# Two decoder layers on one core: attention in rounds between dense products, shared PSUM banks, inverse roots on GpSimd

## The chip, the cores and the metric

The kernel runs on one core of a Trainium2 chip, in one launch. The metric is the device time of that launch in microseconds (us); the kernel before took 696.32 us in the median of three runs (696.04 to 697.86).

In the rows PE is TensorE's matmuls and PEld its weight loads, DVE is VectorE, ACT is ScalarE, POOL is GpSimd, and SP is SyncE, which issues the loads. L221 is line 221 of the kernel.

## The reference

Two layers work on 256 tokens of 1024 features. Each layer is: a mixer, a squared-ReLU MLP, and a per-layer input gated into the residual. Layer 0's mixer is two attentions side by side, layer 1's is one.

```python
def rms_norm(x, g):
    xf = x.astype(jnp.float32)
    y = xf * lax.rsqrt(jnp.mean(xf * xf, axis=-1, keepdims=True) + EPS)
    return (y * g.astype(jnp.float32)).astype(x.dtype)
...
    for i in range(DEPTH):
        hn = rms_norm(h, mix_norm[i])
        mix = even_mixer(...) if i % 2 == 0 else odd_mixer(...)
        h = h + mix
        u = jax.nn.relu(rms_norm(h, ff_norm[i]) @ w_ff1[i])
        h = h + (u * u) @ w_ff2[i]
        g = jax.nn.sigmoid(rms_norm(h, ple_norm[i]) @ w_ple_gate[i])
        h = h + g * (p[i] @ w_ple_proj[i])
```

The even mixer has eight heads of latent attention (MLA: compressed queries of 384 and keys and values of 256, both normalised, heads of 64 plus a rotary part of 32, causal) and eight heads of dilated attention (heads of 64). The odd mixer has 16 heads of 64; with 256 tokens there is one block, so it is causal attention with a distance bias. Queries and keys of every head are normalised by the root of their mean square, and softmax runs over up to 256 keys.

## The kernel before, in words

Every dense product is done in three passes of a reduced fp32 type: weights and activations are split into a high and a low part (`split`, L109 to L111: ScalarE copies the high part, VectorE subtracts it), and high by high, high by low and low by high are added up in PSUM. Weights come in chunks of about 1 MB, in the order of a list; `take` hands out the next chunk and has the two after it loaded and split, a piece of 512 columns at a time, in three buffers.

Activations are feature-major (`feat_mm`, L221: 256 columns to a matmul) or token-major (`tok_mm`, L233: up to 512). Queries, keys and values are token-major products. `heads_norm`, `mla_queries` and `mla_keys` square them on ScalarE, sum on VectorE, take the inverse root (`rsqrt`, L86 to L102), scale, and return a call that transposes the heads on TensorE (`transpose4`, L255) in groups of four, evicted by ScalarE or VectorE.

`rsqrt` is ScalarE's Sqrt, VectorE's reciprocal and, where asked, four more VectorE steps that refine it. Sqrt and Exp are in different tables of ScalarE, so going from one to the other loads a table.

`attn_pair` (L290 to L337) does two heads: their scores in two PSUM banks (L297, L299), bias and row minimum on VectorE (L306), Exp on ScalarE, the row's division on VectorE (L321), three transposes to a head through the one bank named tr (L324), copied by ScalarE (L326), and the products with the values in the bank named o (L330, L333), the first head into rows 0 to 63, the second into rows 64 to 127. Heads of 64 lie two to a tile, in rows 0 to 63 and 64 to 127; MLA heads have 96 rows from row 0. PSUM is 4 banks for dense products (pool pm), 2 for scores (pa), 1 for transposes (pt), 1 for values (po).

What stands in which order on an engine is decided by a scheduler that goes by its own estimate of what is ready first; only the start of layer 0, up to the sums of squares of the residual (L505 to L534), is in written order. The whole attention of a mixer is written behind its products, the per-layer input's projection (`embed`) and the output projection behind it, and the scheduler mixes them.

Of the kernel before, what the change touches and what calls it, by code (L numbers as in the profile page):

```python
# [50 lines left out]
def trunk(ctx, tc, xT, pT, pos, cst, vec, w_c, w_kv, w_dil, w_uq, w_ukv, w_eo,  # L51
# [12 lines left out]
    pt = ctx.enter_context(tc.tile_pool(name="pt", bufs=1, space=PS))  # L64
    po = ctx.enter_context(tc.tile_pool(name="po", bufs=1, space=PS))
# [11 lines left out]
    # the clock gate opens while the first loads are on their way  # L77
# [5 lines left out]
    eps = cp.tile([P, 1], F32, name="eps")  # L83
    V.memset(eps, EPS)

    def rsqrt(y, src, n, refine=False):  # L86
        """y = (src / n + EPS) ** -0.5; n: a number, or one for each src[:, :, i];
        refine: a Newton step on the square root's reciprocal."""
        shp = list(y.shape)
        t = tp.tile(shp, F32, tag=f"nt{shp}", name="nt", bufs=1 if shp[-1] == S else 2)  # L90
        if refine:
            m = tp.tile(shp, F32, tag=f"nm{shp}", name="nm")
# [6 lines left out]
        if refine:  # L99
# [18 lines left out]
    # weights in the order of their use, emitted ahead of it  # L118
# [42 lines left out]
    class Norm:  # L161
        """Gain, split and square sums of the residual, pair of chunks by pair."""
# [40 lines left out]
        def cols(self):  # L203
            """1/rms of every token on all partitions, [128, 256]."""
# [4 lines left out]
            rsqrt(r, ps, D)  # L209
# [5 lines left out]
    def feat_mm(ps, n, wt, x, k0, nk, total, done):  # L215
        """Feature-major: ps[:, j, :] += W[:, tile j].T @ x for k0..k0+nk."""
# [10 lines left out]
    def tok_mm(pss, n, wt, x, k0, nk, total, done):  # L227
        """Token-major: pss[t] += x[:, tokens of t].T @ W for k0..k0+nk."""
# [9 lines left out]
    def tok_group(x, n, nk, kper, late={}, pool=None):  # L238
        """Token-major product; late[i]: calls made before chunk i."""
# [11 lines left out]
    def transpose4(dst, srcs, rows, gain):  # L251
        """Four [128, rows] sources -> dst [rows, 4, 128], times gain."""
# [37 lines left out]
    def attn_pair(heads, mask, mult, dst_hi, dst_lo):  # L290
        """heads: two of (qT [K,256], kT [K,256], v0 [128,64], v1 [128,64], slope)."""
        pts = []
# [7 lines left out]
        for s, (_, _, _, _, slope) in zip(ss, heads):  # L300
# [3 lines left out]
            pr = tp.tile([P, 384], F32, tag="pr", name="pr", bufs=3)  # L304
# [15 lines left out]
            for t, sl in enumerate((slice(0, P), slice(P, 384))):  # L320
                V.tensor_scalar_mul(pr[:, sl], pr[:, sl], rd[:, t:t + 1])  # L321
            ps = pt.tile([P, 384], F32, tag="tr", name="tr")
            for i in range(3):
                T.transpose(ps[:, i * P:(i + 1) * P], pr[:, i * P:(i + 1) * P], ident)  # L324
            pT_ = tp.tile([P, 384], F32, tag="pT", name="pT", bufs=3)
# [10 lines left out]

    def big(shape, dt=F32, name="big"):  # L337
        return bp.tile(shape, dt, tag="b4", name=name)

    def out_proj(mixed, nxt):  # L340
        pss = [pm.tile([P, 2, S], F32, tag="mm", name="mm") for _ in range(4)]
        for kh in range(2):
            for nh in range(2):
                wh, wl = take()
                for j in range(2):
                    c = 2 * nh + j
                    sl = slice(j * 256, (j + 1) * 256)
                    feat_mm(pss[c], 2, (wh[:, :, sl], wl[:, :, sl]), mixed,
                            4 * kh, 4, 8, 4 * kh)
        for c in range(4):  # L350
            hp_ = h[:, 2 * c:2 * c + 2, :]
            V.tensor_add(hp_, pss[c], hp_)
            nxt.pair(c)

    def embed(layer):
        """The per-layer input's projection, feature-major."""
# [5 lines left out]
        es = [big([P, 4, S], name="ple") for _ in range(2)]  # L362
# [5 lines left out]
        return es  # L368
# [121 lines left out]
    def rope(dst, x, tab, t, nh):  # L490
        """dst, x [128, nh, 32]; dst = rotated x."""
# [44 lines left out]
    # gain columns  # L536
# [6 lines left out]
    def compress(pss, n, goff, name):  # L543
        """RMS-normalised latent; the call returned transposes and splits it."""
# [32 lines left out]
    def mla_queries(pss, qT):  # L577
        """Four heads: normalised, rotated; the call returned transposes them."""
# [8 lines left out]
        rsqrt(rs, ms, (64, 32), True)  # L587
# [17 lines left out]
    def mla_keys(pss, kTs):  # L605
        """Eight heads with the shared rotary part; the call returned transposes them."""
# [7 lines left out]
        rsqrt(rs, ms, 64, True)  # L614
# [25 lines left out]
    def rotary_key():  # L640
        kr = tp.tile([P, 2], F32, tag="kr", name="kr", bufs=1)
        rsqrt(kr, km, 32, True)
# [15 lines left out]
    # dilated queries  # L658
# [5 lines left out]
    # MLA queries, keys, values; then dilated keys and values  # L664
# [12 lines left out]
    pss = tok_group(x0, 512, 8, 4, {0: [q0_fin]})  # L677
    dk = big([P, 4, S], name="dk")
    dk_fin = heads_norm(pss, r0, dk, vc[:, V_DK:V_DK + 1])
    pss = tok_group(x0, 512, 8, 4, {0: [q1_fin], 1: [mk_fin, dk_fin]})  # L680
    dv = big([P, 2, 512], name="dv")
    values(pss, r0, dv)

    causal = cs[:, C_CAUSAL:C_CAUSAL + 384]
    for j in range(4):
        hs = []
        for i in range(2):
            hd = 2 * j + i
            sl = slice(hd * 64, (hd + 1) * 64)
            hs.append((mq[hd // 4][:96, hd % 4, :], kTs[hd // 4][:96, hd % 4, :],  # L690
                       mv[:, 0, sl], mv[:, 1, sl], 1.0))
        attn_pair(hs, causal, None, mixed[0][:, j, :], mixed[1][:, j, :])


    def head_pairs(q, k, v, slopes, mask, mult, base):
        for j in range(4):
            hs = []
            for i in range(2):
                hd = 2 * j + i
                sl = slice(hd * 64, (hd + 1) * 64)  # L700
                pr = slice(i * 64, (i + 1) * 64)
                hs.append((q[pr, j, :], k[pr, j, :], v[:, 0, sl], v[:, 1, sl], slopes[hd]))
            attn_pair(hs, mask, mult, mixed[0][:, base + j, :], mixed[1][:, base + j, :])

    head_pairs(dq, dk, dv, [2.0 ** -(i + 1) for i in range(8)],
               cs[:, C_DIL:C_DIL + 384], cs[:, C_MULT:C_MULT + 384], 4)

    es = embed(0)
    nf = Norm(V_FF)
    out_proj(mixed, nf)  # L710
# [5 lines left out]
    # ================= layer 1 =================  # L716
    r1 = None
    x1 = (n1.hi, n1.lo)
    mixed = new_x()
    fin = []  # L720
    for g in range(2):
        pss = tok_group(x1, 512, 8, 4, {1: fin})
        if g == 0:
            r1 = n1.rows()
        q = big([P, 4, S], name="oq")
        fin = [heads_norm(pss, r1, q, goq[:, 4 * g:4 * g + 4])]
        pss = tok_group(x1, 512, 8, 4, {1: fin})
        k = big([P, 4, S], name="ok")
        fin = [heads_norm(pss, r1, k, vc[:, V_OK:V_OK + 1])]
        pss = tok_group(x1, 512, 8, 4, {1: fin})  # L730
        fin = []
        v = big([P, 2, 512], name="ov")
        values(pss, r1, v)
        head_pairs(q, k, v, [2.0 ** (-(8 * g + i + 1) / 2.0) for i in range(8)],
                   cs[:, C_DIST:C_DIST + 384], None, 4 * g)
    es = embed(1)
    nf = Norm(V_FF + 8)
    out_proj(mixed, nf)
# [91 lines left out]
```

## Time and profile before

| what | value |
|---|---|
| median of 3 runs | 696.32 us (696.04 to 697.86) |
| span of the profiled execution | 695.1 us |
| TensorE busy | 684.3 us (98%) |
| VectorE busy | 454.0 us (65%) |
| ScalarE busy | 402.1 us (58%) |
| GpSimd busy | 7.8 us (1%) |
| granted TensorE clock, mean | 0.997 |
| bytes moved | 114.19 MB, 164 GB/s |

The profile gives the span from the first to the last instruction of one execution; the run's time, with what lies around the span, is in the runs, whose median stands 1.2 us above this span. A TensorE that is busy 98% can still be spending time between products: the ends of matmuls are modelled, and a matmul that waits for the one before counts as busy. So the distance from start to start is what counts. The chain of waits gives the work that ended last in order of time: start, duration, engine, what was made and the line.

### The profile page before, as it was taken

Reading aid. Unit: us, or ns where it says so; the run is one execution under the profiler, and the core shown is the slowest. Engines: PE = TensorE matmul, PEld = TensorE weight load, DVE = VectorE, ACT = ScalarE, POOL = GpSimd, SP = SyncE. Lnnn points to the kernel's source line nnn. Section 1 sums busy time; section 2 is a strip of 40 time slices with the busy share of each in tenths; the row PEclk is TensorE's granted clock in tenths of the full one; section 3 lists DMA queues with packets and bytes.
Section 4 is the critical chain, followed back from the end, with each engine's and each line's share of the span. In section 5 each row is a group of like instructions: output and inputs, shape, how many; then the busy total and the mean of one; then the engine's idle time right before and its main releaser. Section 6 shows DMA issues by size and latency. Waiting matters only on the chain.

```text
span 695.1 us, 12543 instructions
## 1 busy us (share of the span) xinstructions
PE 684.3 (98%) x5014; PEld 632.3 (91%) x5014; DVE 454.0 (65%) x1012; ACT 402.1 (58%) x833; POOL 7.8 (1%) x28
## 2 busy tenths in 40 slices
PE   8989999999999999999999999999999999999997
PEld 7878867999999999999988678689999999999997
DVE  5799678686645546557888657648765465564674
ACT  6876776575534435446765765756654354453551
POOL 3100000000000000000000000000000000000000
PEclk9999999999999999999999999999999999999999
DMA  8563610545555554545455235144555545555411
GB/s 257 210 238 136 243 62 5 182 173 188 183 182 182 186 182 178 188 177 183 159 204 182 70 112 197 62 136 167 182 182 190 183 174 194 175 179 197 166 62 61
DMA packets 19066, 114.19 MB, mean 164 GB/s; under 512 B 2240, under 2 KB 4672, under 8 KB 6208
## 3 DMA queue, kind: packets, MB, share of 16 engines
q1 hardware_dynamic: 19008, 113.40, 46.0%
q8 instruction: 39, 0.64, 0.4%
q14 instruction: 19, 0.16, 0.1%
HBM read 112.34 MB, written 1.05 MB: 163 GB/s over the span
## 4 chain that ended last, share of the span: by engine, by line
PE 94%; DVE 2%; DMA 2%; ACT 1%; issue 0%; SPq 0%; POOL 0%; DVEq 0%; ACTq 0%
PE mm L221 42%; PE f L221 27%; PE mm L233 15%; PE o L330 2%; PE tr L324 2%; PE s L299 2%; PE s L297 1%; PE tr L255 1%; DMA raw<-w_c 1%; DMA raw<-w_dil 1%; PE o L333 1%; DVE lo L111 1%; PE st L207 0%; ACT sq L550 0%; ACT L95 0%
## 5 line engine op out<-in xcount | busy, mean ns | idle before, releaser
L110 ACT ACTIVATE hi<-raw 128x512 fp32r<-128x512 f32 (+2 forms) x418 | 241.0, 622 | 212.2 <-PE mm L221 99.9
L111 DVE TENSOR_TENSOR lo<-raw,hi 128x512 fp32r<-128x512 f32 (+2 forms) x418 | 271.5, 685 | 109.6 <-ACT hi L110 109.2
L221 PE MATMUL f<-xh,hi 128*128 128x256 f32 x512 | 145.3, 284 | 0.0
L221 PE MATMUL mm<-uh,hi 128*128 128x256 f32 x512 | 144.9, 283 | 0.0
L221 PE MATMUL mm<-ul,hi 128*128 128x256 f32 x512 | 144.9, 283 | 0.0
L221 PE MATMUL mm<-uh,lo 128*128 128x256 f32 x512 | 144.9, 283 | 0.0
L221 PE MATMUL f<-xh,lo 128*128 128x256 f32 x512 | 144.9, 283 | 0.0
L221 PE MATMUL f<-xl,hi 128*128 128x256 f32 x512 | 144.9, 283 | 0.0
L221 PEld LDWEIGHTS f<-xl,hi 128*128 128x128 f32 x512 | 98.3, 192 | 0.1
L221 PEld LDWEIGHTS f<-xh,hi 128*128 128x128 f32 x512 | 98.3, 192 | 0.1
L221 PEld LDWEIGHTS mm<-uh,hi 128*128 128x128 f32 x512 | 98.3, 192 | 0.0
L221 PEld LDWEIGHTS mm<-ul,hi 128*128 128x128 f32 x512 | 98.3, 192 | 0.0
L221 PEld LDWEIGHTS mm<-uh,lo 128*128 128x128 f32 x512 | 98.3, 192 | 0.0
L221 PEld LDWEIGHTS f<-xh,lo 128*128 128x128 f32 x512 | 98.3, 192 | 0.0
L221 PE MATMUL mm<-xh,hi 128*128 128x256 f32 x256 | 73.0, 285 | 0.0
L221 PE MATMUL mm<-xl,hi 128*128 128x256 f32 x256 | 73.0, 285 | 0.0
L221 PE MATMUL mm<-xh,lo 128*128 128x256 f32 x256 | 72.8, 285 | 0.0
L233 PE MATMUL mm<-hi,xh 128*128 128x512 f32 (+1 forms) x160 | 63.3, 398 | 1.2 <-ACT hi L110 1.2
L233 PE MATMUL mm<-lo,xh 128*128 128x512 f32 (+1 forms) x160 | 63.2, 395 | 0.5 <-DVE lo L111 0.5
L233 PE MATMUL mm<-hi,xl 128*128 128x512 f32 (+1 forms) x160 | 62.5, 390 | 0.0
L391 DVE SCALAR_TENSOR_TENSOR u<-f,cr 128x512 f32<-128x512 f32 x32 | 22.1, 691 | 52.4 <-PE f L221 52.4
L221 PEld LDWEIGHTS mm<-xh,hi 128*128 128x128 f32 x256 | 49.0, 192 | 0.8 <-issue 0.8
(189 smaller groups left out, 876.1 us busy)
## 6 DMA issues: line engine op xcount, KB each, us to landing
raw<-w_f SPq DMA_DIRECT2D x64, 1024.0 KB, 4.8
raw<-w_odd SPq DMA_DIRECT2D x12, 1024.0 KB, 4.9
raw<-w_g SPq DMA_DIRECT2D x8, 1024.0 KB, 4.9
raw<-w_dil SPq DMA_DIRECT2D x6, 1024.0 KB, 5.7
raw<-w_eo SPq DMA_DIRECT2D x4, 1024.0 KB, 5.7
raw<-w_oo SPq DMA_DIRECT2D x4, 1024.0 KB, 4.9
raw<-w_p SPq DMA_DIRECT2D x2, 1024.0 KB, 4.9
raw<-w_c SPq DMA_DIRECT2D x8, 208.0 KB, 3.8
```

Source lines behind the costliest of these rows:

```text
L110: A.activation(hi, src, AF.Copy)
L111: V.tensor_sub(lo, src, hi.bitcast(F32))
L221: T.matmul(ps[:, j, :], lhsT=a[:, kk, j * P:(j + 1) * P], rhs=b[:, k0 + kk, :], start=(done == 0 and kk == 0 and j == 0 and i == 0), stop= ...
L233: T.matmul(pss[t][:, :n], lhsT=a[:, k0 + kk, t * P:(t + 1) * P], rhs=b[:, kk, :], start=(done + kk == 0 and i == 0), stop=(done + kk == to ...
L255: T.transpose(ps[:rows, i, :], s, ident)
L297: T.matmul(s[:, :P], lhsT=qT[:, :P], rhs=kT[:, :P], start=True, stop=True)
L299: T.matmul(s[:, P:], lhsT=qT[:, P:], rhs=kT, start=True, stop=True)
L324: T.transpose(ps[:, i * P:(i + 1) * P], pr[:, i * P:(i + 1) * P], ident)
L330: T.matmul(o[i * 64:(i + 1) * 64, :], lhsT=heads[i][2], rhs=pts[i][:, :S], start=True, stop=False, skip_group_check=True)
L333: T.matmul(o[i * 64:(i + 1) * 64, P:], lhsT=heads[i][3], rhs=pts[i][:, S:], start=False, stop=True, skip_group_check=True)
L391: V.scalar_tensor_tensor(u, ps, 0.0, rb[0], op0=OP.max, op1=OP.mult)
```

## The change

- `attn_pair` becomes three functions: scores and softmax, transposes, values. `attention` calls them in rounds: the transposes of the last pair, the scores of the next, one unit of a dense product, the values of the last pair, and then some more units (a list says how many).
- The dense products beside them become generators whose units are 6 matmuls of 512 columns or 12 of 256: in layer 0 the dilated keys and values and the per-layer input beside the MLA pairs, and the output projection beside the dilated pairs; in layer 1 the second group's products beside the first group's pairs, and the per-layer input and output projection beside the second's.
- In these stages TensorE's order is the written one (`manual_schedule(engines={PE})`); the other engines keep the scheduler.
- The pools pt and po become one pool of two banks, for transposes, values and sums.
- Small inverse roots become a multiply and add, and a power of -0.5, both on GpSimd (the first on VectorE where the source is in PSUM). The refinement goes. The four roots over whole rows (`rsqrt_row`, 256 columns) stay as they were.
- Around the output projection the squares of the residual are written behind all four of its ends.

```diff
-    pt = ctx.enter_context(tc.tile_pool(name="pt", bufs=1, space=PS))
-    po = ctx.enter_context(tc.tile_pool(name="po", bufs=1, space=PS))
+    pt = ctx.enter_context(tc.tile_pool(name="pt", bufs=2, space=PS))
...
+    def rsqrt(y, src, n):
+        t = tp.tile(list(y.shape), F32, tag=f"nt{list(y.shape)}", name="nt")
         for i, num in enumerate(n if isinstance(n, tuple) else (n,)):
             ix = (slice(None), slice(None), i) if isinstance(n, tuple) else slice(None)
-            A.activation(t[ix], src[ix], AF.Sqrt, scale=1.0 / num, bias=eps[:, 0:1])
-            if refine:
-                V.tensor_scalar(m[ix], src[ix], 1.0 / num, EPS, op0=OP.mult, op1=OP.add)
+            (V if src.space == PS else G).tensor_scalar(t[ix], src[ix], 1.0 / num, EPS,
+                                                       op0=OP.mult, op1=OP.add)
...
+        G.tensor_tensor(y, t, e.to_broadcast(list(y.shape)), op=OP.pow)
...
-        V.reciprocal(y, t)
-        if refine:
-            V.scalar_tensor_tensor(t, y, -0.5, y, op0=OP.mult, op1=OP.mult)
-            V.tensor_mul(t, t, m)
-            V.scalar_tensor_tensor(y, t, 1.5, y, op0=OP.add, op1=OP.mult)
...
-        o = po.tile([P, S], F32, tag="o", name="o")
+        o = pt.tile([P, S], F32, tag="tr", name="o")
...
+    def attention(pairs, mask, mult, mixed, base, dense, units):
+        prs, pts = {}, {}
+        for i, n in enumerate(units):
+            if i > 0:
+                pts[i - 1] = attn_transpose(prs.pop(i - 1))
+            if i < 4:
+                prs[i] = attn_scores(pairs[i], mask, mult)
+            run(dense, 1)
+            if i > 0:
+                attn_values(pairs[i - 1], pts.pop(i - 1), mixed[0][:, base + i - 1, :],
+                            mixed[1][:, base + i - 1, :])
+            run(dense, n)
...
+    def dense0():
+        yield from tok_units(x0, 512, 8, 4,
+                             lambda p: fins.append(heads_norm(p, r0, dk, vc[:, V_DK:V_DK + 1])),
+                             {2: [q0_fin], 4: [mk_fin], 6: [q1_fin]})
+        yield from tok_units(x0, 512, 8, 4, lambda p: values(p, r0, dv),
+                             {4: [lambda: fins.pop()()]})
+        yield from embed_units(0, es)
...
+    with tc.manual_schedule(engines={mybir.EngineType.PE}):
+        dense = dense0()
+        run(dense, 7)
+        attention([mla_pair(j) for j in range(4)], cs[:, C_CAUSAL:C_CAUSAL + 384], None,
+                  mixed, 0, dense, [2, 2, 2, 2, 1])
+        run(dense)
...
+        attention([pair(dq, dk, dv, sl8, j) for j in range(4)], cs[:, C_DIL:C_DIL + 384],
+                  cs[:, C_MULT:C_MULT + 384], mixed, 4, dense, [2, 1, 1, 1, 1])
```

TensorE in layer 1, first group of heads, before: mm is the dense product of the first keys and values, s the scores, tr the transposes of softmax rows, o the products with values.

```order
L297 MATMUL s<-ok,oq 128x128
L299 MATMUL s<-ok,oq 128x256
L297 MATMUL s<-ok,oq 128x128
L299 MATMUL s<-ok,oq 128x256
L233 MATMUL mm<-hi,xl 128x512
...
L324 MATMUL tr<-cs,pr 128x128 x3
L233 MATMUL mm<-lo,xh 128x512
L297 MATMUL s<-ok,oq 128x128
L299 MATMUL s<-ok,oq 128x256
L233 MATMUL mm<-hi,xl 128x512
L324 MATMUL tr<-cs,pr 128x128 x3
L330 MATMUL o<-pT,ov 64x256
```

The same place after, one round with the dense product of the second group:

```order
L331 MATMUL tr<-cs,pr 128x128 x6
L298 MATMUL s<-ok,oq 128x128 x2
L300 MATMUL s<-ok,oq 128x256 x2
L233 MATMUL mm<-hi,xh 128x512
L233 MATMUL mm<-lo,xh 128x512
L233 MATMUL mm<-hi,xl 128x512
...
L340 MATMUL o<-pT,ov 64x256 x2
L343 MATMUL o<-pT,ov 64x128 x2
```

The scores and values of single heads between dense matmuls have become one group of transposes and scores and one of values, each of both heads.

TensorE in layer 0 at the transposes of the MLA keys (kf are the key tiles), before, where dk's and dv's products are mm:

```order
L255 MATMUL tr<-cs,kf 96x128 x4
L233 MATMUL mm<-hi,xl 128x512
L233 MATMUL mm<-hi,xh 128x512
L233 MATMUL mm<-lo,xh 128x512
...
L255 MATMUL tr<-cs,kf 96x128 x4
```

After, between the fourth and the fifth unit of dk's product:

```order
L233 MATMUL mm<-hi,xh 128x512
L233 MATMUL mm<-lo,xh 128x512
L233 MATMUL mm<-hi,xl 128x512
L255 MATMUL tr<-cs,kf 96x128 x16
L233 MATMUL mm<-hi,xh 128x512
```

Four groups of four, which stood in the product that follows, have become one block of sixteen in the middle of the product before it.

GpSimd behind the rope tables, before and after (rr are the inverse roots of the residual and the two latents, kr of the rotary key, rs of the heads):

```order
L484 TENSOR_TENSOR tcos_289<-co,vc 128x2x16
L485 TENSOR_TENSOR tsin_290<-ns,vc 128x2x16
L486 TENSOR_TENSOR tsin_290<-sn,vc 128x2x16
L825 UNCONDITIONAL_BRANCH
L825 ISA
```

```order
L565 TENSOR_TENSOR tsin_289<-ns,vc 128x2x16
L566 TENSOR_TENSOR tsin_289<-sn,vc 128x2x16
L97 TENSOR_TENSOR rr<-nt,mhalf 128x2
L92 TENSOR_SCALAR nt<-rm 128x2
L97 TENSOR_TENSOR rr_370<-nt,mhalf 128x2
L92 TENSOR_SCALAR nt<-rm 128x2
L92 TENSOR_SCALAR nt<-km 128x2
L97 TENSOR_TENSOR rr_386<-nt,mhalf 128x2
L97 TENSOR_TENSOR kr<-nt,mhalf 128x2
```

GpSimd had nothing to do after the tables; now every small inverse root of the kernel goes through its queue, the first behind the tables.

## Rows read from the trace of the kernel before

**Rows 1.** The page's first part: busy us, share of the span, instructions

```profile
PE 684.3 (98%) x5014; PEld 632.3 (91%) x5014; DVE 454.0 (65%) x1012; ACT 402.1 (58%) x833; POOL 7.8 (1%) x28
```

**Rows 2.** The chain of waits in order of time: start, us, what

```profile
49.52 4.61 PE mm L233 x12
54.13 0.44 PE tr L255 x4
...
80.77 0.45 PE s L297 x4
81.22 0.87 PE s L299 x4
...
140.37 5.76 PE f L221 x48
...
146.99 40.30 PE f L221 x336
...
349.42 10.91 PE mm L233 x48
360.32 0.79 PE st L196 x8
...
368.31 0.44 PE tr L255 x4
...
481.20 5.76 PE f L221 x48
```

**Rows 3.** Timeline of TensorE: start, us, line, operation, out and in, shapes

```profile
384.75 0.39 PE L233 MATMUL mm<-hi,xl 128*128 128x512 f32 x1
385.07 0.49 PE L297 MATMUL s<-ok,oq 64*128 64x128 f32 x4
...
385.92 0.50 PE L233 MATMUL mm<-hi,xh 128*128 128x512 f32 x1
386.26 0.40 PE L233 MATMUL mm<-lo,xh 128*128 128x512 f32 x1
```

**Rows 4.** Timeline of TensorE a little later, same columns

```profile
392.38 0.65 PE L330 MATMUL o<-pT,ov 128*64 128x256 f32 x2
392.96 0.48 PE L297 MATMUL s<-ok,oq 64*128 64x128 f32 x2
...
393.81 0.43 PE L330 MATMUL o<-pT,ov 128*64 128x256 f32 x1
393.81 0.43 PE L333 MATMUL o<-pT,ov 128*64 128x128 f32 x2
...
394.60 0.55 PE L324 MATMUL tr<-cs,pr 128*128 128x128 f32 x3
```

**Rows 5.** Groups by line and form: count, busy us, mean ns, idle before

```profile
L111 DVE TENSOR_TENSOR lo<-raw,hi 128x512 fp32r<-128x512 f32 x400 | 258.9, 684 | 107.4 <-ACT hi L110 107.2
...
L257 ACT ACTIVATE mk<-tr,gc 96x512 f32<-96x512 f32 x4 | 2.7, 682 | 1.1 <-PE tr L255 1.1
```

**Rows 6.** Who TensorE waited for: us in total, times, longest

```profile
PE mm L233 <- DVE rp L595: 2.0, 1, 2.0
```

**Rows 7.** Stretch 49.50 to 53.30: length, busy by engine, granted clock, DMA

```profile
49.50:53.30 3.80, 3.77 (x10) 2.99 (x11) 3.12 (x15) 0.61 (x2) 0.00 (x0) 0.55 0.57 241
```

**Rows 8.** GpSimd's groups by line and form, columns as in rows 5

```profile
L453 POOL TENSOR_SCALAR ang<-vc,posf 128x16 f32<-128x16 f32 x2 | 1.4, 692 | 0.1
L465 POOL TENSOR_TENSOR ang<-ang,rt 128x32 f32<-128x32 f32 x4 | 1.1, 264 | 0.3
```

**Rows 9.** Timeline of GpSimd and ScalarE at the first inverse root

```profile
26.03 0.25 POOL L486 TENSOR_TENSOR tsin<-sn,vc 128x32 f32<-128x32 f32 x1
...
26.26 0.46 ACT L635 ACTIVATE krope<-mm,rr 128x32 f32<-128x32 f32 x2 [0.23 <-DVE rr L98]
```

**Rows 10.** Timeline of VectorE before and at the last MLA key tile

```profile
54.29 0.25 DVE L98 RECIPROCAL rs<-nt 128x16 f32<-128x16 f32 x1 [1.67 <-ACT nt L95]
...
65.23 0.21 DVE L622 COPY kf<-krr 128x128 f32<-128x128 f32 x1
```

More of the change, by code (lines that the diff above doesn't have):

```diff
@@ new lines, in run, with tok_units @@
+    def run(dense, n=None):
+        while n is None or n > 0:
+            if next(dense, run) is run:
+                return
+            n = None if n is None else n - 1
+    def tok_units(x, n, nk, kper, done, late={}):
+        pss = [pm.tile([P, 512], F32, tag="mm", name="mm") for _ in range(2)]
+        for k in range(nk):
+            for f in late.get(k, ()):
+                f()
+            if k % kper == 0:
+                wh, wl = take()
+            kk = slice(k % kper, k % kper + 1)
+            tok_mm(pss, n, (wh[:, kk], wl[:, kk]), x, k, 1, nk, k)
+            if k == nk - 1:
+                done(pss)
+            yield
@@ L337, in big, with out_units, unit @@
     def big(shape, dt=F32, name="big"):
         return bp.tile(shape, dt, tag="b4", name=name)
-    def out_proj(mixed, nxt):
-        pss = [pm.tile([P, 2, S], F32, tag="mm", name="mm") for _ in range(4)]
-        for kh in range(2):
-            for nh in range(2):
[L344 to L350, printed above, removed]
+    def out_units(mixed, pss):
+        def unit(wt, nh, kk, kh):
+            for j in range(2):
+                sl = slice(j * 256, (j + 1) * 256)
+                feat_mm(pss[2 * nh + j], 2, (wt[0][:, kk:kk + 1, sl], wt[1][:, kk:kk + 1, sl]),
+                        mixed, 4 * kh + kk, 1, 8, 4 * kh + kk)
+        pss += [pm.tile([P, 2, S], F32, tag="mm", name="mm") for _ in range(4)]
+        for nh in range(2):
+            wt = take()
+            for kk in range(4):
+                unit(wt, nh, kk, 0)
+                yield
+        wts = [take(1), take(1)]
+        pss.append(wts)
+        for kk in range(2):
+            for nh in range(2):
+                unit(wts[nh], nh, kk, 1)
+                yield
@@ L351, in out_proj, with out_proj_end, part, end @@
+    def out_proj_end(mixed, pss, nxt):
+        wts = pss[4]
+        def part(c, kk):
+            sl = slice((c % 2) * 256, (c % 2 + 1) * 256)
+            wh, wl = wts[c // 2]
+            feat_mm(pss[c], 2, (wh[:, kk:kk + 1, sl], wl[:, kk:kk + 1, sl]),
+                    mixed, 4 + kk, 1, 8, 4 + kk)
+        def end(c):
             hp_ = h[:, 2 * c:2 * c + 2, :]
             V.tensor_add(hp_, pss[c], hp_)
-            nxt.pair(c)
-    def embed(layer):
+            nxt.split(2 * c)
+            nxt.split(2 * c + 1)
+        part(0, 2)
+        part(1, 2)
+        for c in range(4):
+            if c > 1:
+                part(c, 2)
+            part(c, 3)
+            end(c)
+        for c in range(4):
+            nxt.square(c)
@@ L357, in embed, with embed_units @@
+    def embed_units(layer, es):
         praw = tp.tile([P, 2, S], F32, tag="z", name="praw", bufs=ZB)
@@ L361, in embed @@
         wh, wl = take()
-        es = [big([P, 4, S], name="ple") for _ in range(2)]
+        es += [big([P, 4, S], name="ple") for _ in range(2)]
         for c in range(4):
@@ L676, in trunk, with mla_pair, pair @@
         A.activation(mv[:, t, :], pss[t][:, :512], AF.Copy)
[L677 to L685, printed above, removed]
+    dk, dv = big([P, 4, S], name="dk"), big([P, 2, 512], name="dv")
+    fins, es = [], []
+    def dense0():
[5 more added lines that the diff above has]
+        yield from embed_units(0, es)
+    def mla_pair(j):
+        hs = []
+        for hd in (2 * j, 2 * j + 1):
+            sl = slice(hd * 64, (hd + 1) * 64)
+            hs.append((mq[hd // 4][:96, hd % 4, :], kTs[hd // 4][:96, hd % 4, :],
+                       mv[:, 0, sl], mv[:, 1, sl], 1.0))
+        return hs
+    def pair(q, k, v, slopes, j):
         hs = []
@@ L689, in trunk @@
             sl = slice(hd * 64, (hd + 1) * 64)
[L690 to L710, printed above, removed]
+            pr = slice(i * 64, (i + 1) * 64)
+            hs.append((q[pr, j, :], k[pr, j, :], v[:, 0, sl], v[:, 1, sl], slopes[hd]))
+        return hs
+    with tc.manual_schedule(engines={mybir.EngineType.PE}):
[4 more added lines that the diff above has]
+        run(dense)
+        sl8 = [2.0 ** -(i + 1) for i in range(8)]
+        pss = []
+        dense = out_units(mixed, pss)
+        attention([pair(dq, dk, dv, sl8, j) for j in range(4)], cs[:, C_DIL:C_DIL + 384],
+                  cs[:, C_MULT:C_MULT + 384], mixed, 4, dense, [2, 1, 1, 1, 1])
+        run(dense)
+        nf = Norm(V_FF)
+        out_proj_end(mixed, pss, nf)
     ng = Norm(V_PLE)
@@ L714, in trunk, with group, first, dense1 @@
     gate(ng, es, n1)
-    r1 = None
     x1 = (n1.hi, n1.lo)
+    r1 = []
     mixed = new_x()
[L720 to L730, printed above, removed]
-        fin = []
[L732 to L738, printed above, removed]
+    qkv = [(big([P, 4, S], name="oq"), big([P, 4, S], name="ok"), big([P, 2, 512], name="ov"))
+           for _ in range(2)]
+    def group(g):
+        q, k, v = qkv[g]
+        fin = []
+        def first(pss):
+            if not r1:
+                r1.append(n1.rows())
+            fin.append(heads_norm(pss, r1[0], q, goq[:, 4 * g:4 * g + 4]))
+        late = {4: [lambda: fin.pop()()]}
+        yield from tok_units(x1, 512, 8, 4, first)
+        yield from tok_units(x1, 512, 8, 4, lambda p: fin.append(
+            heads_norm(p, r1[0], k, vc[:, V_OK:V_OK + 1])), late)
+        yield from tok_units(x1, 512, 8, 4, lambda p: values(p, r1[0], v), late)
+    def dense1():
+        yield from embed_units(1, es)
+        yield from out_units(mixed, pss)
+    with tc.manual_schedule(engines={mybir.EngineType.PE}):
+        run(group(0))
+        for g in range(2):
+            if g == 0:
+                dense, units = group(1), [3, 3, 3, 3, 3]
+            else:
+                es, pss = [], []
+                dense, units = dense1(), [2, 2, 2, 2, 1]
+            run(dense, 2)
+            sl8 = [2.0 ** (-(8 * g + i + 1) / 2.0) for i in range(8)]
+            attention([pair(*qkv[g], sl8, j) for j in range(4)], cs[:, C_DIST:C_DIST + 384],
+                      None, mixed, 4 * g, dense, units)
+            run(dense)
+        nf = Norm(V_FF + 8)
+        out_proj_end(mixed, pss, nf)
     ng = Norm(V_PLE + 8)
```

38 lines of the change are left out of this document (24 added, 14 removed).

## The prediction

> **What bounds the kernel now.** I read the page's busy shares first, then the chain of waits in order of time, then the timeline of TensorE in the attention stretches, and last the order of the instructions before and after. The shares say that TensorE is busy 98% of the span [rows 1]; the reader is to see there that no other engine can be the bound, and that a change can only win by giving TensorE less to do, or fewer of its few stops. The chain says what TensorE does at its best: 336 matmuls of 256 columns in 40.30 us, 0.120 each, and 48 of 512 columns in 10.91 us, 0.2273 each [rows 2]. All of the two MLPs and gates runs at that pace, and the change touches nothing of it. What is left is the mixers: in layer 0 from 54.13, where the transposes of the first MLA queries begin, to 140.37, where the MLP begins (86.2 us), and in layer 1 from 349.42 to 481.20 (131.8 us) [rows 2].
>
> Taken apart, layer 1's stretch holds 288 matmuls of 512 columns (65.5 us), 240 of 256 (the embedding's 48 and the output projection's 192: 28.8 us), the row sums (0.8 us) and eight groups of four transposes of normalised heads. Leaving the dense product and coming back to it costs time of its own: before the scores at 385.07 the last dense matmul takes 0.32 us instead of 0.227, and the one at 385.92 takes 0.34 [rows 3], so 0.09 and 0.11. A group of four is 0.44 [rows 2] and this 0.20, so 0.64, eight of them 5.1. There remain 131.8 - 65.5 - 28.8 - 0.8 - 5.1 = 31.6 us for eight head pairs, 3.95 each. Layer 0 in the same way: 96 matmuls of 512 (21.8), 240 of 256 (28.8), ten groups (6.4), so 29.2 us for eight pairs, 3.65 each.
>
> The timeline shows where a pair's time goes. The scores of two heads issued together take 385.07 to 385.92, 0.85 us [rows 3]; those of one head alone take 392.96 to 393.81, the same 0.85 [rows 4]. The heads lie on different 64 rows, and side by side they cost one. The order of before puts most heads apart, and the value products of a pair in two pieces, 0.58 and 0.79 us [rows 4].
>
> **The change part by part.** *Rounds.* In the new order a round is: six transposes of the last pair, the four score matmuls of the next, one dense unit, the four value matmuls, more dense units. So the scores are always side by side, and there are two excursions from the dense product in a pair. Six transposes at a quarter of 0.44 each [rows 2] and one change of form are 0.75. Scores 0.85. Values together: bounded above by 0.58 + 0.79 less one change, 1.27; below by one head alone, 0.58 for its long matmul and half of that for its short one, 0.87. At 393.81 a matmul of one head and one of the other start at the same moment [rows 4], so I take 0.95, near the lower end. Two excursions 0.40. Sum 2.95 us. An MLA pair has 96 rows to a head and no room for two: its scores are 0.45 + 0.87 = 1.32 [rows 2], its sum 3.42. Layer 1: 8 x 2.95 = 23.6 instead of 31.6, -8.0 us. Layer 0: 4 x 3.42 + 4 x 2.95 = 25.5 instead of 29.2, -3.7 us.
>
> At 393.81 the trace shows the two heads' value matmuls starting together, but in a mixed order. The Trainium skill (TensorE: Matmul & The Clock Gate, Part 3: Packing small matmuls) says that matmuls whose outputs lie in different column groups run at the same time, as those in different row groups do. By the rows values cost 0.87 to 1.27; by that rule they are at the 0.87 and the sum is 16 x 0.08 = 1.3 us lower.
>
> *Transposes of normalised heads.* They now stand eight together, once sixteen. Layer 1: four blocks at 0.88 + 0.20 = 4.3 instead of 5.1, -0.8. Layer 0: 40 transposes in four blocks, 4.4 + 0.8 = 5.2 instead of 6.4, -1.2. With two banks for them, a block of sixteen is paced by ScalarE's copies at 0.68 each [rows 5]: about 0.5 us longer, counted below.
>
> *Small inverse roots.* One stop of before disappears. At 47.5 TensorE waits 2.0 us for VectorE to empty the banks of the first MLA queries [rows 6], and the 12 matmuls behind it take 4.61 us instead of 2.73 [rows 2], at a mean granted clock of 0.55, so mostly at the lower of its two levels, 1.2 GHz, after that stop [rows 7]. That emptying stands behind ScalarE's square root, a reciprocal and four refinement steps, interleaved with weight splitting, and behind the transposes of the key latents, which the new order does first. The new path is two multiplies and one power on GpSimd. I take -2.0 - 1.9 = -3.9; what ends last there then is the dense product itself.
>
> No row here runs a power. GpSimd's rows of this size run from 0.264 (a product of 128x32) to 0.692 us (the first of its kind) [rows 8]; a power can hardly be cheaper than the product, and I keep three times the slowest row, 2 us, as the upper end. I take 0.5 us, near those rows. At the start it costs time: GpSimd's rope tables last until 26.28 [rows 9], the first power is queued behind them, and the ScalarE work that used to begin at 26.26 [rows 9] begins at about 26.8; the compressed queries then need a second multiply and power in place of a root and a reciprocal, 0.5 more. Their transposes now stand three matmuls earlier in TensorE's queue, so they stop all dense work behind them: +1.0 us, between 0.5 and 4.
>
> *The fixed order.* In these stages TensorE no longer takes what is ready; it follows the written order, and everything behind a waiting matmul waits. Two places count. (a) The sixteen transposes of the MLA keys stand after four units of the dilated keys. In before the last key tile was finished at about 65.4 [rows 10]. The dilated keys' product began behind the transposes at 54.13, so at about 54.6; TensorE now comes to the key tiles at 54.6 - 3.9 + 1.0 + 4 x 6 x 0.2273 + 1.1 (eight query transposes) = 58.3. VectorE has three weight pieces less ahead of it (2.0 us), twelve small refinement steps less (an estimate: 0.1 us each), and no 1.67 us wait for a root [rows 10]; and its queue starts some 2 us earlier, since the stop at 47.5 is gone: about 58.5. I take +1.0 with the 0.5 of the copies, between 0 and 5. (b) The 16 rounds. From scores to transposes the softmax has two dense units and the values, some 4 us, and shares VectorE with weight splitting, 0.684 us a piece [rows 5]. VectorE's and ScalarE's queues are in order, so a piece ahead of the softmax delays the next transposes and all behind them. Between none and one piece a round, 0 to 11 us; I take 0.4 a round, +6.4.
>
> The trace shows the clock at half after the one 2.0 us stop. The Trainium skill (TensorE: Matmul & The Clock Gate, Part 1: The HAM clock gate) says that the array falls to 1.2 GHz when it has been idle and has to be busy to get back, which speaks against a fixed order with waits in it. By the rows, waits of 0.4 us amid matmuls cost only themselves; by that rule a stop at (a) of the old size would cost 1.9 us once more. No run here shows it for the new order.
>
> Loads keep their order except that layer 1's per-layer input is issued one weight chunk earlier; it is needed after the second group, so I count nothing.
>
> *Sum.* -8.0 - 3.7 - 0.8 - 1.2 - 3.9 + 1.0 + 1.0 + 6.4 = -9.2. The profiled span of 695.1 us becomes 685.9. The median of the runs, 696.3, is 1.2 above that span, and I add these: **687.1 us**.
>
> **The rivals.** *The power is slow* (slower than before). A power of p us adds e = p - 0.5 at each place where nothing hides it: twice at the start, twice at layer 1's first queries (their transposes follow after four units, 5.5 us, nearly all of it needed), about 0.7 e at its first keys, some 3 e through VectorE's queue before the MLA keys, and 1.5 e in the rounds whose heads are normalised beside them: about 9 e. The gain of 9.2 is gone at e = 1.0, p = 1.5; slower by more than 0.3% from p = 1.8; at p = 4 it is 687.1 + 31 = 718 us. For it: no row shows a power, and GpSimd's first multiplies took 0.692. Against it: the tiles have 2 to 16 columns, and the rows of twice that size take a quarter of a us.
>
> *The rounds starve.* The softmax is late by one weight piece or more in every round. VectorE and ScalarE have room on average, but at the dilated pairs of layer 0, with one unit between, the softmax has an extra multiplication by the mask's counts. Then +11 instead of +6.4, and with the key transposes at 4: 687.1 + 4.6 + 3 = 694.7, barely faster.
>
> *The value products do not overlap.* 16 x 0.32 = 5.1 more: 692.2.
>
> *Nothing waits.* Without (a) and (b): 679.7; with the values at 0.87 as well 678.4.
>
> **How the numbers follow.** The forecast's own terms, within half of the waits either way (682 to 692): 0.50. Nothing waits (677 to 682): 0.18. Starved rounds, alone or with values that don't overlap (692 to 698): 0.20. Slow power (over 698): 0.12. A measurement of this kernel can tell about 0.3%, 2.1 us, from no change: faster is below 694.2. Of the third case I give half to that side, and a little of it goes over the upper bound: faster 0.77, same 0.10, slower 0.13. The range from 677 to 698 leaves out the slow power and little else.
>
> **What would show it.** In the profile after: TensorE's score rows in pairs and no single head; layer 1's stretch from the gate's end to the MLP at about 126 us and layer 0's from the dilated keys' start to the MLP at about 83; no stop of 2 us ahead of the MLA values and no stretch at half clock there; GpSimd rows of the power of about 0.5 us. The prediction is wrong if the waits of TensorE for the transposes' inputs add up to more than 11 us, if a power takes over 1.5 us, or if a pair still costs TensorE 3.5 us without waiting.

## The result and the profile after

The changed kernel takes 706.13 us (median of 4 runs, 705.39 to 709.99) against 696.52 us (696.04 to 697.86) for the kernel before, measured beside it: ratio 1.014, 95% interval 1.011 to 1.017. It is slower by 9.6 us; 687.1 was predicted, faster by 9. Of the rivals it is the slow power that the profile and the experiments below bear out.

The page's first part, which answers to [rows 1]:

```profile
PE 673.2 (96%) x5014; PEld 629.0 (89%) x5014; DVE 450.1 (64%) x983; ACT 392.4 (56%) x813; POOL 43.0 (6%) x56
```

TensorE is busy 11 us less than before, though some of that time now runs at half clock, so its own work did get shorter. But the span grew from 695.1 to 704.5: it now stands still more. GpSimd's busy time rose from 7.8 to 43.0 us. The page's chain of waits by engine:

```profile
PE 80%; DVE 8%; POOL 5%; ACT 3%; DMA 2%; issue 1%; SPq 1%; POOLq 0%; DVEq 0%; ACTq 0%
```

GpSimd, idle for nearly the whole of the kernel before, now holds 5% of the chain, about 35 us. Its costliest groups by line and form (count, busy us, mean ns, idle before) say with what; they answer to [rows 8]:

```profile
L97 POOL TENSOR_TENSOR rs<-nt,mhalf 128x16 f32<-128x16 f32 x9 | 26.9, 2990 | 0.8
L97 POOL TENSOR_TENSOR rr<-nt,mhalf 128x2 f32<-128x2 f32 x4 | 3.2, 801 | 279.1 <-DVE nt L92 279.0
L92 POOL TENSOR_SCALAR nt<-ms 128x16 f32<-128x16 f32 x7 | 3.1, 439 | 83.5 <-DVE ms L270 77.9 <-DVE ms L692 5.6
```

A power of 16 columns takes 2.99 us, one of 2 columns 0.80. Nine of the wide ones stand in chains, here the one at the start of layer 1 in order of time (start, us, what):

```profile
355.38 10.91 PE mm L233 x48
366.28 0.80 PE st L196 x8
...
367.34 1.10 POOL rr L97
...
368.47 0.70 ACT sq L268
...
369.19 1.29 DVE ms L270 x2
...
370.55 0.58 POOL nt L92
...
371.21 2.90 POOL rs L97
...
374.31 0.60 DVE lo L111
374.92 0.61 DVE z L276
...
375.57 0.67 PE tr L255 x4
```

From the end of the row sums to the transposes of the first heads it is 8.5 us, 4.6 of them on GpSimd (1.10, 0.58, 2.90). TensorE has four units of the next product to do meanwhile, 24 x 0.2273 = 5.5 us [rows 2], and then stands for 2.9 us, the longest wait of the second row below. Who TensorE waited for (us in total, times, longest):

```profile
PE tr L255 <- DVE xl L111: 5.5, 3, 2.9
PE tr L255 <- DVE z L276: 4.1, 2, 2.9
PE mm L233 <- DVE lo L111: 3.6, 5, 1.5
PE tr L648 <- issue: 2.2, 1, 2.2
PE tr L255 <- DVE ckl L653: 2.1, 1, 2.1
PE mm L233 <- DVE rp L675: 1.9, 2, 1.3
PE tr L255 <- DVE kf L699: 1.8, 1, 1.8
```

All entries of this view together are 25.7 us, against 5.8 us in the kernel before. Of the rows shown only z, rp and kf are made from a power. The waits for xl, lo and ckl are for splits (of attention values, of weights, of the key latents), which need none; they stand in VectorE's queue behind instructions that wait for one. So at 423.58, the longest wait of the first row: the pair's scores were done at 416.2, but VectorE waited for a power until 417.07 and only at 420.16 came to their mask, and the split of attention values that TensorE then waits for was done more than 3 us after that. The row of L648 is the start: the transposes of the latents come 2.2 us late, after VectorE waited 5.7 us there for the small powers behind the rope tables. The same view for VectorE:

```profile
DVE rs L273 <- POOL rs L97: 18.0, 6, 3.3
...
DVE z L672 <- POOL rs L97: 6.1, 2, 3.3
...
DVE kf L699 <- POOL rs L97: 3.1, 1, 3.1
```

All nine wide powers leave VectorE standing, 27.2 us together; in the six of the first row the instruction right behind the waiting one does not need the power. VectorE's timeline shows one:

```profile
41.18 0.34 DVE L653 SCALAR_TENSOR_TENSOR ckl<-tr,vc,ckh 128x128 fp32r<-128x128 f32 x1
44.24 0.17 DVE L273 TENSOR_TENSOR rs<-rs,rr 128x16 f32<-128x16 f32 x1 [2.71 <-POOL rs L97]
...
44.50 1.28 DVE L276 TENSOR_TENSOR z<-mm,rs 128x512 f32<-128x512 f32 x2
...
45.80 0.34 DVE L653 SCALAR_TENSOR_TENSOR ckl<-tr,vc,ckh 128x128 fp32r<-128x128 f32 x1
```

The second split of the key latents (ckl) stands behind the 2.71 us wait, and TensorE's transposes, which start at 46.19, waited 2.1 us until it was done. These transposes read the z of the line above, made from the power between 44.50 and 45.78, so the split itself adds at most 1 us of the 2.1. After some of the stops the granted clock is at half, 1.2 GHz, in three stretches (columns as in [rows 7]):

```profile
55.30:62.10 6.80, 5.96 (x14) 4.65 (x15) 3.46 (x10) 3.13 (x7) 3.85 (x3) 0.50 0.43 154
376.20:379.60 3.40, 3.37 (x11) 2.88 (x11) 3.33 (x6) 0.00 (x0) 0.00 (x0) 0.50 0.54 154
424.00:427.40 3.40, 3.40 (x11) 2.73 (x9) 3.10 (x6) 0.75 (x2) 0.00 (x0) 0.51 0.12 48
```

That is 13.6 us at half; before it was 3.4, about the stretch of [rows 7] (both without the last two microseconds of the span). The Trainium skill (TensorE: Matmul & The Clock Gate, Part 1: The HAM clock gate) says that an idle array falls to 1.2 GHz; the prediction set that rule beside the order, and the stretches here agree with it. Not every stop brings one: behind the 2.1 us before 46.19 the clock stayed at 2.4 GHz.

The rounds themselves came out as written. One of layer 1, from the chain:

```profile
458.76 0.66 PE tr L331 x6
459.42 0.42 PE s L298 x4
459.84 0.43 PE s L300 x4
460.27 1.63 PE mm L221 x12
461.90 0.58 PE o L340 x4
462.48 0.22 PE o L343 x4
462.70 3.06 PE mm L221 x24
465.76 0.66 PE tr L331 x6
```

A round is 465.76 - 458.76 = 7.00 us with 36 dense matmuls at 0.120 in it (4.32), so this pair costs 2.68; 2.95 was predicted, 3.95 was the price before. The MLPs begin here, which answers to the rows of 140.37 and 481.20 in [rows 2]:

```profile
146.16 6.12 PE f L221 x51
...
490.02 6.12 PE f L221 x51
```

Layer 0 ends its mixer 5.8 us later than before, and layer 1's mixer takes 490.02 - 355.38 = 134.6 us instead of 131.8, 2.8 more. The rest of the kernel is within 0.8 us. So the mixers lost 8.6 us where 9.2 were to be won, and the difference is looked for in the experiments.

### The profile page after: what moved, and what is told of

Read it like the earlier page. It is cut to its first block, busy times and chain, and to the rows that moved or that the text cites. A ratio compares the mean times of both kernels' runs of the same rounds, so it can differ in the third digit from the quotient of the medians.

```text
span 704.5 us, 12505 instructions
## 1 busy us (share of the span) xinstructions
PE 673.2 (96%) x5014; PEld 629.0 (89%) x5014; DVE 450.1 (64%) x983; ACT 392.4 (56%) x813; POOL 43.0 (6%) x56
## 4 chain that ended last, share of the span: by engine, by line
PE 80%; DVE 8%; POOL 5%; ACT 3%; DMA 2%; issue 1%; SPq 1%; POOLq 0%; DVEq 0%; ACTq 0%
PE mm L221 40%; PE f L221 26%; PE mm L233 8%; POOL rs L97 3%; DVE lo L111 2%; PE tr L331 1%; DVE ms L270 1%; PE tr L255 1%; DMA raw<-w_kv 1%; PE s L300 1%; PE o L340 1%; DVE z L276 1%; PE s L298 1%; ACT hi L110 1%; DVE sc L307 1%
## 5 line engine op out<-in xcount | busy, mean ns | idle before, releaser
L221 PE MATMUL mm<-xh,hi 128*128 128x256 f32 x256 | 74.5, 291 | 0.0
L233 PE MATMUL mm<-hi,xh 128*128 128x512 f32 (+1 forms) x160 | 66.6, 416 | 1.4 <-ACT hi L110 1.4
```

What stands on the lines that cost most here:

```text
L221: T.matmul(ps[:, j, :], lhsT=a[:, kk, j * P:(j + 1) * P], rhs=b[:, k0 + kk, :], start=(done == 0 and kk == 0 and j == 0 and i == 0), stop= ...
L233: T.matmul(pss[t][:, :n], lhsT=a[:, k0 + kk, t * P:(t + 1) * P], rhs=b[:, kk, :], start=(done + kk == 0 and i == 0), stop=(done + kk == to ...
```

## The experiments

Ratios are to the kernel before, run on the same chip beside each; times in us are compared across chips, on which the kernel before took 696.5 to 698.1 us in the median.

**e1: the roots of before, everything else of the change kept.**

```
-            (V if src.space == PS else G).tensor_scalar(t[ix], src[ix], 1.0 / num, EPS,
-                                                       op0=OP.mult, op1=OP.add)
...
-        G.tensor_tensor(y, t, e.to_broadcast(list(y.shape)), op=OP.pow)
+            A.activation(t[ix], src[ix], AF.Sqrt, scale=1.0 / num, bias=eps[:, 0:1])
...
+        V.reciprocal(y, t)
+        if refine:
+            V.scalar_tensor_tensor(t, y, -0.5, y, op0=OP.mult, op1=OP.mult)
...
```

> The kernel after, with the small inverse roots of before (square root on ScalarE, reciprocal and, where before had it, the refinement on VectorE); the rounds and the two shared banks stay. Theory 'slow power' (the 128x16 power takes 2.99 us on GpSimd where 0.5 was taken, nine of them, and TensorE's order waits behind most): 686 to 694 us, about 10 to 20 under the kernel after, at most one stretch at half clock before the MLP of layer 0. Theory 'starved rounds' (VectorE and ScalarE cannot deliver in time for an order that is written out, whatever the root costs): 702 to 710 us, since three more table loads of 1.28 us come back. Theory 'shared banks' (transposes wait for the bank that the values hold): 700 to 706, the wait of the transposes for the split of the values stays at 5 us.

687.29 us, ratio 0.987 (0.984 to 0.991). Taking the power out gives back 18.8 us and turns the change into a gain. The chain of e1 at the same places:

```profile
137.71 6.12 PE f L227 x51
...
346.91 10.92 PE mm L239 x48
...
471.38 6.12 PE f L227 x51
```

Layer 0's mixer ends 2.7 us earlier than before, layer 1's takes 124.5 us, 7.3 less. "Starved rounds" and "shared banks" fall: the same order and the same banks are fast with another root, although ScalarE loads eight more tables than in the kernel after (15 of 1.28 us against 7; the expectation had three). The rows of xl and ckl, and those of lo before the products mm, are gone from the list of TensorE's waits, which adds up to 11.5 us, 14.2 less than in the kernel after. And 10.2 us less lie at half clock, where a matmul of 512 columns takes 0.43 us from start to start (at 58.01 in the kernel after) and not 0.227, so nearly 5 us were lost there. Together that is 19 us, an estimate, for the 18.8 measured.

**e2: the power alone, in the kernel before.**

```
-            A.activation(t[ix], src[ix], AF.Sqrt, scale=1.0 / num, bias=eps[:, 0:1])
...
+        G.tensor_tensor(y, t, e.to_broadcast(list(y.shape)), op=OP.pow)
```

> The kernel before, with only the small roots changed to a power on GpSimd; no rounds, TensorE's order left to the scheduler. 'Slow power': the nine chains grow by about 1.5 us each and most are waited for, 701 to 710 us. 'Starved rounds' and 'shared banks' (the power is not to blame): 694 to 699 us, as before.

720.25 us, ratio 1.034 (1.031 to 1.037): 22.6 us for the power alone, more than any theory gave it. The expectation took 1.5 us more at each place. By the rows it is more: a wide power with its multiply is 2.99 + 0.44 = 3.43 us, the old root 0.32 (square root of 128x16) + 0.25 (reciprocal) = 0.57 in the trace of e1, so 2.9 more, and nine of them make 26, less some 2 us for the four small steps of refinement (0.17 each) that three of the nine had. An order written out for TensorE plays no part in it: here the scheduler made it.

**e4: each power issued twice.**

```
         G.tensor_tensor(y, t, e.to_broadcast(list(y.shape)), op=OP.pow)
+        G.tensor_tensor(y, t, e.to_broadcast(list(y.shape)), op=OP.pow)
```

> The kernel after, with each power issued twice in a row (the second writes the same values), so each of nine chains is 3.0 us longer and each of five small ones 0.8. 'Slow power': all of it shows, 9 x 3.0 + 4 x 0.8 = 30 us, less what work fills: 724 to 738 us. 'Starved rounds' or 'shared banks': under 5 us, 706 to 711.

742.84 us, ratio 1.067 (1.063 to 1.070): 36.7 us above the kernel after, for 31 us more of GpSimd, and above the expected 724 to 738. TensorE's waits add up to 49.7 us instead of 25.7, so 24 of the 31 us show as stops. The rest is probably clock, which I did not separate: the mean granted clock is 0.963 instead of 0.990, and 54.6 us of the span lie at 1.2 GHz. Who TensorE waits for is the list of after, with nearly every entry from a power grown:

```profile
PE tr L256 <- DVE z L277: 19.0, 5, 6.7
PE mm L234 <- DVE lo L112: 6.4, 3, 5.0
```

So little else hides the power; it is on the path nearly everywhere.

**e6: the power stays, the transposes of normalised heads come three units later.**

```
-                             {2: [q0_fin], 4: [mk_fin], 6: [q1_fin]})
+                             {2: [q0_fin], 4: [q1_fin], 6: [mk_fin]})
...
-                             {4: [lambda: fins.pop()()]})
+                             {7: [lambda: fins.pop()()]})
...
-        late = {4: [lambda: fin.pop()()]}
+        late = {7: [lambda: fin.pop()()]}
```

> The kernel after, with the transposes of normalised heads three units later in TensorE's order (before unit 7 of the next product instead of unit 4; the keys of MLA before unit 6 and its second queries before unit 4). The power stays on GpSimd. 'Slow power': the waits of line 255 for the normalised heads (z 4.1, kf 1.8 us) and most of those for banks (5.5) go, with the half clock behind two of them: 692 to 698 us. 'Starved rounds': 703 to 708, the waits move to other places. 'Shared banks': the transposes of 8 meet the banks at another place, 702 to 708.

696.76 us, ratio 1.000 (0.998 to 1.002). The sum is as expected, its parts are not. The chain:

```profile
356.36 10.91 PE mm L233 x48
...
480.39 6.12 PE f L221 x51
```

Layer 1's mixer takes 124.0 us, less than in e1: three units more (18 x 0.2273 = 4.1 us) cover its four wide powers but for a wait of 1.3 us for a split. Layer 0 gained nothing (its MLP starts at 147.14, 1.0 later than after): its powers delay the MLA products ahead of the rounds, which this edit does not touch.

**e8: e6 with the roots of e1; e9: e8 with the power in layer 1 alone; e11: e8 without the refinement of the MLA roots** (e11 leaves out that Newton step, nothing else). In e9 `root` is the old one, used by all callers of layer 0; e11's whole root is the last piece.

```
-            rsqrt(r, ps, D)
+            (rsqrt if self.off == V_MIX + 8 else root)(r, ps, D)
...
+            A.activation(t[ix], src[ix], AF.Sqrt, scale=1.0 / num, bias=eps[:, 0:1])
+        V.reciprocal(y, t)
```

> The kernel after with the small roots of before (as in e1) and the later transposes (as in e6). If what e1 left (TensorE waiting for dk 1.0, oq 0.8, z 0.6, kf 0.5 us at the transposes of heads) was due to the place of the transposes: 683 to 686 us. If those waits only move: 686 to 689, as e1.

> As e8, but layer 1's five roots (one of 2 columns, four of 16) are powers on GpSimd; layer 0 has the roots of before. 'Slow power, hidden': with the transposes three units later nothing waits for the four powers of 16 columns, so only the one of 2 columns shows: within 1.5 us of e8. 'Slow power through VectorE's queue' (VectorE stands in order behind the power, and weight splits behind it come late): 4 x 1.5 = 6 us above e8, 690 to 693.

> As e8, without the refinement of the MLA roots (square root and reciprocal alone). It takes four small VectorE operations each from three chains in layer 0, some 12 x 0.17 = 2 us of VectorE ahead of the MLA banks: 1 to 3 us under e8 if that chain is waited for, the same if not.

683.86 us (ratio 0.980, 0.977 to 0.982), 684.38 (0.980, 0.978 to 0.982) and 681.29 (0.977, 0.975 to 0.979). All as the first branch of each said. e9 sets a price on a covered power: layer 1's stretch is 468.31 - 344.26 = 124.05 us with powers and 468.27 - 344.95 = 123.32 without, 0.7 for four wide ones and a narrow one. The queue of VectorE still shows in it: at the one place in layer 1 where heads' transposes wait, it is 1.3 us for a split with the powers (e9) and 0.8 for the copy of the group before without (e8):

```profile
PE tr L273 <- DVE xl L129: 1.3, 1, 1.3
```

```profile
PE tr L261 <- DVE oq L265: 0.8, 1, 0.8
```
e11 shows what the refinement costs: layer 0's MLP starts 2.9 us earlier (132.78 against 135.73).

**e12: the power by itself, at seven widths, with products beside it, added to e1.**

```
+    for w in (1, 2, 4, 8, 16, 32, 64):
+        G.tensor_tensor(scr[:, 1, :w], scr[:, 0, :w],
+                        mhalf[:, 0:1].to_broadcast([P, w]), op=OP.pow)
...
```

> e1 with fourteen extra GpSimd instructions on scratch at the start of layer 0's MLP, where GpSimd has nothing else to do: a power and a product of 128x1, 2, 4, 8, 16, 32 and 64 each. 'Price by the column': 0.49 + 0.156 per column, from 0.80 us at 2 and 2.99 at 16, so 0.65, 0.80, 1.1, 1.7, 3.0, 5.5 and 10.5 us; the products 0.2 to 0.35. 'Price by the call' (a set-up cost that made 16 columns dear): 32 and 64 columns cost little more than 16, 3 to 4 us.

687.11 us (one run), as e1. GpSimd's groups by line and form (the power is L808, the product L810):

```profile
L808 POOL TENSOR_TENSOR scr<-scr,mhalf 128x64 f32<-128x64 f32 x1 | 10.5, 10516 | 0.0
L808 POOL TENSOR_TENSOR scr<-scr,mhalf 128x32 f32<-128x32 f32 x1 | 5.4, 5410 | 0.0
L808 POOL TENSOR_TENSOR scr<-scr,mhalf 128x16 f32<-128x16 f32 x1 | 3.1, 3132 | 0.0
...
L810 POOL TENSOR_TENSOR scr<-scr,mhalf 128x64 f32<-128x64 f32 x1 | 1.0, 1004 | 0.0
...
L808 POOL TENSOR_TENSOR scr<-scr,mhalf 128x2 f32<-128x2 f32 x1 | 0.7, 712 | 0.0
...
L808 POOL TENSOR_TENSOR scr<-scr,mhalf 128x1 f32<-128x1 f32 x1 | 0.6, 576 | 74.3 <-DVE scr L806 74.3
```

The price goes by the column: (10.516 - 0.576) / 63 = 0.158 us each, on 0.42 for the call. The products do not follow their width: 0.19, 0.20, 0.69, 0.26, 0.83, 1.55 and 1.00 us from 1 to 64 columns, four of the seven above the expected 0.2 to 0.35, and no run shows why. At every width the power is dearer, by 1.5 times at 4 columns and ten times at 64.

**e13: e1 with one bank for transposes and one for values; e14: the kernel before with two shared banks only.**

```
-    pt = ctx.enter_context(tc.tile_pool(name="pt", bufs=2, space=PS))
+    pt = ctx.enter_context(tc.tile_pool(name="pt", bufs=1, space=PS))
+    po = ctx.enter_context(tc.tile_pool(name="po", bufs=1, space=PS))
```

> e1 (rounds, roots of before) with the banks of before: one bank for transposes and one for values, instead of two that both share. If the shared pair matters to the rounds: each of the sixteen rounds has two tiles of transposes (for two heads) and one of values, so with one bank the second head's transposes wait for ScalarE's copy of the first (0.54 us or more): 16 x 0.5 = 8 us above e1, 693 to 697. If it doesn't (the second copy is waited for anyway): 686 to 689, as e1.

> The kernel before with two shared banks only; no rounds, no powers. If the banks bring time by themselves: 690 to 694 us (the transposes of a pair's heads no longer wait for one copy). If only the rounds use them: 695 to 699, as before.

e13 takes 718.2 us, ratio 1.030 (1.028 to 1.033), 31 us more than e1 and far above both branches; e14 697.43, ratio 1.001 (1.000 to 1.003), as before. So the shared pair is worth nothing to the old program and everything to the rounds. In e13:

```profile
PE tr L338 <- ACT pT L340: 15.8, 16, 2.5
```

In each of 16 rounds the second head's transposes wait for the copy of the first, on the mean 1 us, twice what was expected. That is half of the 31 us. TensorE's waits add up to 34.8 us, 23.3 more than in e1, so some 7 more are other waits (head transposes for copies, for example); clock may be the rest (17 us at half before the end, against 3.4 in e1), and I did not take it apart further.

**e15: e1, and e16: the kernel after, with TensorE's order in the mixers left to the scheduler** (the code and its order of emission unchanged).

```
-    with tc.manual_schedule(engines={mybir.EngineType.PE}):
+    if True:
```

> e1 with the order of TensorE's instructions in the two mixers left to the scheduler (same code and rounds, but what it holds ready first comes first). If the gain of e1 is that of the fixed rounds (heads side by side): it is lost, 693 to 699 us. If the gain is that of the new order of the code, whoever schedules it: 685 to 690.

> The kernel after (powers on GpSimd, rounds, two shared banks) with TensorE's order in the two mixers left to the scheduler, as in e15. If the written order is what makes TensorE wait for the powers: 690 to 698 us, most of the 20 us between e1 and the kernel after is gone. If the powers cost as much in any order that was made before their price was known (e2 says so for the kernel before): 702 to 712.

e15: 684.30 us, ratio 0.983 (0.981 to 0.985), 3 us under e1 (0.987, 0.984 to 0.991), at the edge of what the two intervals tell apart. Layer 1's stretch is 121.9 us (by the chain, 346.04 to 467.90), 2.6 less than in e1. My first branch falls, and the second's range is missed by 0.7 us on the fast side: the gain does not need the order written out for TensorE, the code of the rounds is enough. e16: 704.87 us, ratio 1.010 (1.007 to 1.013), 20.6 above e15. The power costs 18.8 us in the written order, 20.6 in the scheduler's (18.6 and 19.1 by the ratios), 22.6 in the old program: the written order is not its cause.

## Why the prediction was wrong

**The step that failed** is the price of the small inverse roots: "I take 0.5 us, near those rows", with 2 us, "three times the slowest row", as the upper end. Measured: 0.80 at 2 columns, 2.99 at 16, above my upper end, which rested on nothing that computes a power. The rows I took it from are of other operations (the 0.264 that I called a product is a sum, line 465; the tables' products take 0.25). My argument against the rival, that rows of twice the size "take a quarter of a us", says nothing of a power, which grows by 0.158 us with each column. With the measured price my own rival gives e = 2.49, 9 e = 22.4, 709.5 us; the runs gave 706.1. So the places at which the power shows were counted about right, though the 687.1 under that sum came out by luck (below). The break-even (p = 1.5) no run tested; the chance of 0.12 was low for a price that no row bounds.

**Rounds.** With the roots of before the kernel takes 687.3 (e1) where the terms gave 687.1, but that is luck: the pairs brought more than I priced, the rounds did not wait, and the stop that I had written off stayed. Layer 1: -5.6 by my terms (-8.0, -0.8, +3.2), -7.3 measured. Layer 0: -3.6 by my terms, -2.7 measured.

- A pair costs 2.68 us, not 2.95: the values of two heads take 0.58 + 0.22 = 0.80 where I took 0.95, and six transposes 0.66 where I took 0.75. The Trainium skill (TensorE: Matmul & The Clock Gate, Part 3: Packing small matmuls) says that different column groups run at the same time; the trace agrees, and the lower end of my bounds, 0.87, was still too high. In e1 a round beside matmuls of 512 columns takes 8.22 us with 24 of them in it (5.46), so 2.77; two rounds of MLA pairs take 7.14 with 18 of 512 columns (4.09) and 7.26 with 36 of 256 (4.32), so 3.05 and 2.94, not 3.42; a dilated round takes 5.55 with 24 of 256 (2.88), so 2.67. At these prices the pairs bring 9.8 us in layer 1 and 6.5 in layer 0, 4.6 more than I had.
- The 16 rounds' waits were priced too high: +6.4. In e1 no wait of TensorE for the softmax reaches the list, whose smallest entry is 0.3 us; "starved rounds" is refuted. The +1.0 for the MLA keys was near: e1 waits 0.5 for kf and 1.3 for their copies. At the other transposes of heads, for which I had no term, it waits 2.4 (dk 1.0, oq 0.8, z 0.6). The +1.0 for the start is the 2.2 us before L648 in the kernel after; with the old roots it is not in the list.
- The stop that was to disappear did not. I priced -3.9. In the kernel after TensorE waits 1.9 us for rp there (L675), 1.5 for a late split, and then runs 6.8 us at half clock. With the old root (e1) it is there too, longer than before's 2.0 us, with 3.4 us at half clock as before:

```profile
PE mm L239 <- DVE rp L681: 3.3, 1, 3.3
```

Without the refinement it is 1.6 in e11, and no stretch before the last microseconds lies at half clock. So the reason given (the root's refinement in front of the emptying) was sound in part, worth 2.6 us between e8 and e11; the power put back as much of a stop (1.9 + 1.5 against 3.3) and twice the time at half clock.

**What I did not price.** That the rounds depend on the two shared banks (31 us by e13). It did not show in the result, since both came together.

**What was to show it.** The first sign of being wrong, a power of over 1.5 us, is there. The second, waits for the transposes' inputs of more than 11 us, is there only if the waits for splits are counted in: z and kf are 5.9, with xl and ckl 13.5. The third, a pair at 3.5 us, is not. Layer 1's stretch is 134.6 us instead of about 126, layer 0's 85.6 (60.57 to 146.16) instead of about 83, and there is a stretch at half clock where none was to be.

## What to carry to other kernels

An operation that no row shows has no price: the rows of its neighbours bound the call, not the work for each element, so before it is put nine times onto chains that products wait for, time it alone at its real width, as e12 does in one run. And ask what is queued behind the instruction that waits for it: here VectorE stood for all nine powers, and weight splits with no root in them were late. Where a slow step must stay, move its reader: three units of dense work covered the 3 us powers of layer 1 (e6), at 0.7 us for all of them (e9).

## What the runs showed that was not expected

GpSimd's power costs 0.158 us for each column of 128 rows, where a product of 64 columns is done in 1.0 us (e12). A slow step can cost more than its length: twice the powers put 31 us on GpSimd and 36.7 on the kernel, with the time at half clock going from 13.6 to 54.6 us. The scheduler, given the code of the rounds, made an order at least as good as the written one (684.3 against 687.3, near the edge of the intervals). And the fastest version here is neither kernel: rounds, shared banks, late transposes and plain square roots take 681.3 us, 2.3% under the kernel before (2.1 to 2.6).
